# Hybrid decoder layer on one core: the transposes of the last attention gate placed inside the first output unit, seven-product pairs at places 3 to 13

## The chip, the core and the metric

The kernel runs on one core of a Trainium2 chip. TensorE (PE) multiplies matrices, VectorE (DVE) and ScalarE (ACT) work elementwise, GpSimd (POOL) and SyncE (SP) here only issue DMAs. The metric is the device time of one execution in microseconds, lower is better. Before the change it is 1550.36 us, the median of 3 runs (1549.83 to 1550.70).

## What is computed

One decoder layer on 256 tokens of width 4096, in float32: an RMS norm, one input projection to eight parts, three mixers (pooling, stick-breaking attention, a state space), each normalised and gated, and one output projection with the residual, then a last RMS norm.

```python
def hybrid_layer(x, ...):
    h = rmsnorm(x, ln_g)
    p_x, p_gate, q, k, v, a_gate, s_u, s_gate = jnp.split(h @ w_in, ...)
    y_pool = pool_mixer(p_x, ...)
    y_attn = stick_breaking_attention(q, k, v)
    y_ssm = s5_mixer(s_u, ...)
    y_pool = rmsnorm(y_pool, g_pool) * jax.nn.silu(p_gate)
    y_attn = rmsnorm(y_attn, g_attn) * jax.nn.silu(a_gate)
    y_ssm = rmsnorm(y_ssm, g_ssm) * jax.nn.silu(s_gate)
    y = jnp.concatenate([y_pool, y_attn, y_ssm], axis=-1)
    return x + y @ w_out
```

## The kernel before

The weights are cut into pieces of 128 x 2 x 512 numbers (512 KB). A list `subs` holds all 528 pieces in the order of use, and one loop walks through it. In each step the loop issues the loads that come due (on SP's queue, four pieces ahead, six in the output part), splits the piece after next into a high and a low part, and issues the step's matmuls. The split is `hi_lo`: ACT makes `hi` as a rounded copy, the DVE makes `lo` as the difference. A product in float32 is three matmuls (hi x hi, lo x hi, hi x lo), so a plain piece takes 12 matmuls: two rows of the piece, two token halves, three products. The split parts lie in a ring of 4 buffers, 6 in the output part.

The pieces form units. 24 input units and 4 GLU units come first, the last of them the four units `ag` of the attention gate. Then come four output units `out`, each 16 places `s` with two pieces (`h` = 0, 1) and 1024 columns of the result. In an output unit some places, listed in `SEVEN`, multiply their two pieces as a 2 x 2 block with seven products instead of eight: 21 matmuls instead of 24, for which `split_seven` makes four sums of weight halves (the tile named `t`, in a loop of its own on the DVE), and `row_sums` makes three sums of the token side (`ts`, then the split `y`). `row_difference` overwrites a half of the place's rows with a difference, so such a place can no longer be multiplied plainly. The products `p7` (four halves of PSUM banks, printed as `p`) gather over all such places of a unit, and `join_seven` adds them up (the tile `e`) after the last one, then into `o`; at the end of the unit `finish` adds the accumulator `pm` to `o`.

The stationary side of the output units is `xhl`, 32 slots of 128 channels, split. The gated branches `y` are transposed on TensorE (`transposed`, 8 transposes in two halves `h`) into a PSUM tile `ps_t`. The first seven groups of four slots go to DRAM (`kept`) and come back in the last `ag` unit (`take_back`, tile `yk`, at every second step of it). The last attention gate (`ag` unit 3) has no time for that: `direct` writes slots 28 to 31 from `ps_t` straight into `xhl`. They are read by the places 14 and 15.

That gate is a generator, `att_gate`, with four steps: load `ya` and form the sigmoid `sgm` on ACT and DVE; multiply into `ya`; first half of the transposes; second half. Generators stand in `side_q`; `pump` runs steps of the first one, `drain` runs all to their end. Before the change, `drain(side_q)` stands directly behind the last `ag` unit's matmuls. Engines other than SP take their instructions in the order that a scheduler gives at build time; SP takes them as written. Within an engine the order is kept at run time, so an instruction that waits holds up all behind it.

PSUM has 8 banks. In the output part four tiles `b0` to `b3` of two banks each divide them: unit `n` gathers in two of them (`pm`) and puts its seven products (`p7`) in the other two, and the next unit swaps the pairs. The first output unit takes `b0`, `b1` for `pm`, over the banks of the `ag` units' accumulators.

The buffers tagged `k4` (six) are shared by `agz`, `ya`, `sgm`, `yk`, the sums `t7`, `fg` and `e7`.

At the very end, the last `HELD` = 4 pieces are multiplied for the first token half only, and for the second half after that, so that the first half's result is normalised and stored while TensorE still works.

Of the kernel before, what the change touches and what calls it, by code (L numbers as in the profile page):

```python
# [12 lines left out]
F32 = mybir.dt.float32  # L13
# [7 lines left out]
P = 128  # L21
L = 256
D = 4096
KT = D // P
NU = 512
# [9 lines left out]
RING_OUT = 6  # L35
K4 = 6
LATE_AT = 15
SEVEN = (2, 4, 6, 8, 10, 12)
WIDE = 2 * NU
WARM = 8  # L40
SQUARE_AT = (0, 1, 3, 4, 6, 7, 9, 10)
# [17 lines left out]
OUT_FROM = 24 * 16 + 4 * 4  # L59
# [3 lines left out]
def body(tc, a, out, ctx):  # L63
    nc = tc.nc
# [18 lines left out]
    bp = pool("base")  # L83
# [74 lines left out]
    def hi_lo(dst_hi, dst_lo, src):  # L158
        made = act(dst_hi, src, AF.Copy)
        tt(dst_lo, src, dst_hi.bitcast(F32), ALU.subtract)  # L160
        return made
# [10 lines left out]

    def seven(i):
        ui, s, h = subs[i]
        return units[ui][0] == "out" and s in SEVEN

    def flat(w):
        return w.rearrange("p k n -> p (k n)")
# [61 lines left out]
    def row_sums(where, kept_in, s, xa, xb):  # L240
        t = where.tile([P, 3, P], F32, tag="t", bufs=1, name="ts")
        tt(t[:, 0, :], xa[:, P:L], xb[:, P:L], ALU.add)
        tt(t[:, 1, :], t[:, 0, :], xa[:, 0:P], ALU.subtract)
        tt(t[:, 2, :], xb[:, 0:P], t[:, 1, :], ALU.subtract)
        y = where.tile([P, 3, 2, P], F32R, name="y7_%d" % s)
        hi_lo(y[:, :, 0, :], y[:, :, 1, :], t)
        kept_in[s] = y

    def row_difference(xa):
        tt(xa[:, P:L], xa[:, 0:P], xa[:, P:L], ALU.subtract)  # L250
# [13 lines left out]
    state = {"s7_out": {}, "out": False}  # L264
# [33 lines left out]

    def transposed(y, emit):
        for h in range(2):  # L300
            ps = pk.tile([P, 512], F32, tag="ps", bufs=2, name="ps_t")
            for c in range(2):
                for t in range(2):
                    T.transpose(ps[:, (c * 2 + t) * P:(c * 2 + t + 1) * P], y[:, t, (h * 2 + c) * P:(h * 2 + c + 1) * P], ident)  # L304
            for c in range(2):
                emit(h * 2 + c, ps[:, c * L:c * L + L])
            yield
# [19 lines left out]
    def take_back(g):  # L327
        t = bp.tile([P, 4, L], F32, tag="k4", bufs=K4, name="yk")
        nc.sync.dma_start(t, kept[g])
        for h in range(2):  # L330
            s = 2 * g + h
            if s in SEVEN:
                row_sums(state["out_rows"], state["s7_out"], s, t[:, 2 * h, :], t[:, 2 * h + 1, :])
                row_difference(t[:, 2 * h, :])
        hi_lo(xhl[:, 4 * g:4 * g + 4, 0, :], xhl[:, 4 * g:4 * g + 4, 1, :], t)

    def square_sums(dst, y, n):
        junk = mp.tile([P, 512], BF16, tag="junk", bufs=1, name="junk")
# [366 lines left out]
    def pump(q, n):  # L705
        while q and n > 0:
            try:
                if next(q[0], "end") == "end":
                    q.popleft()
                    continue  # L710
            except StopIteration:
                q.popleft()
                continue
            n -= 1

    def drain(q):
        pump(q, 1 << 30)
# [47 lines left out]

    def start_end():
        nonlocal ep
        drain(side_q)
        late_ctx.close()
        psum_ctx.close()  # L770
        ep = end_ctx.enter_context(tc.tile_pool(name="end", bufs=1, side="right", reuse_waits="tile"))
        state["o"] = ep.tile([P, 2, D], F32, name="o")
        state["po"] = end_ctx.enter_context(tc.tile_pool(name="pout", bufs=1, space=PSUM, reuse_waits="tile"))
        state["out"] = True

    def start_out(n):
        if n == 0:
            start_end()
        four = [state["po"].tile([P, 2, NU], F32, tag="b%d" % j, bufs=1, name="pm" if j // 2 == n % 2 else "p7") for j in range(4)]
        c, p = four[n % 2 * 2:n % 2 * 2 + 2], four[2 - n % 2 * 2:4 - n % 2 * 2]  # L780
        o = state["o"][:, :, n * WIDE:n * WIDE + WIDE]
        for h in range(2):
            nc.sync.dma_start(o[:, :, h * NU:h * NU + NU], a["xr"][2 * n + h])
        return c, p, o

    def load_fg(n):
        fg = bp.tile([P, WIDE], F32, tag="k4", bufs=K4, name="fg")
# [91 lines left out]
    for i, (ui, s, h) in enumerate(subs):  # L879
        kind, c, nk = units[ui]  # L880
        if ui == 1 and s == 0:
            constants()
        if ui == 1 and s in SQUARE_AT:
            square_x(SQUARE_AT.index(s))
        if ui == 1 and s == 12:
            with tc.high_priority():
                norm_x()
                take_u(scaled(state.pop("ps0"), "suz"), 0)
        if s == 0 and h == 0:
            if ui == LATE_AT:  # L890
                start_late()
            if kind == "out":
                ps, pp, state["o_n"] = start_out(c)
                pp = [pp[j // 2][:, j % 2, :] for j in range(4)]
            else:
                ps = [pm.tile([P, NU], F32, tag="c%d" % t, bufs=2, name="pm") for t in range(2)]
            if kind == "glu" and hhl is None:
                hhl = split_glu()
        while loaded < min(len(subs), i + 1 + LOAD_AHEAD + (2 if state["out"] else 0)):
            if loaded == 0:  # L900
                load_first()
            else:
                if loaded < KT // 2:
                    load_x(loaded)
                load(loaded)
            loaded += 1
        while split_to < min(len(subs), i + 1 + SPLIT_AHEAD):
            split(split_to)
            split_to += 1
        if kind == "ag" and c == A_G + 1536 and s >= 2 and s % 2 == 0:  # L910
            take_back(s // 2 - 1)
        rows = hhl if kind == "glu" else xhl
        if seven(i):
            if h == 0:
                mm_seven(i, s, ps, pp, s == SEVEN[0], s == SEVEN[-1])
                if s == SEVEN[-1]:
                    state["fg"] = load_fg(c)
                    state["joined"] = join_seven(pp, state["o_n"])
        else:
            pair = htiles.pop(i)  # L920
            late = i >= N_SUB - HELD
            into = [ps[t][:, h, :] for t in range(2)] if kind == "out" else ps
            mm_tok(into, rows, (2 * s, 2 * s + 1), pair, s == 0, s == nk // 2 - 1, (0,) if late else (0, 1))
            if late:
                delayed.append((s, h, pair))
        if s == nk // 2 - 1 and h == (1 if kind == "out" else 0):
            n = nth.get(kind, 0)
            nth[kind] = n + 1
            if (kind, n) != ("out", 3):
                finish(kind, c, n, ps)  # L930
            if kind == "ag" and n == 3:
                drain(side_q)
        pump(side_q, 3)
        if i >= SSM_FROM:
            want = (i - SSM_FROM) * SSM_RATE
            while ssm_steps[0] < want and ssm_q:
                pump(ssm_q, 1)
                ssm_steps[0] += 1
# [121 lines left out]
```

## Time and profile before

| | |
|---|---|
| median of 3 runs | 1550.36 us |
| the profiled execution | 1550.4 us |
| its span in the trace | 1548.6 us |
| mean granted clock of TensorE | 0.992 |
| last matmul of the last `ag` unit starts | 1180.80 us |
| first matmul of the first output unit starts | 1198.66 us |
| end of the output units' matmuls | 1537.2 us |

The span is what the trace covers; the 1.8 us between it and the time lie around it. Busy times of engines run side by side. A row of the timeline has start, duration, engine, line, operation, written tile <- read tiles, shapes, a count, and in brackets the idle time before it with what ended it. Durations overlap a little: the next instruction of an engine starts before the former one's end, so the cost of a row is the distance between starts. A row of the stretches (windows) has the stretch, its length, the busy times of the engines with counts, the granted clock, the DMA share and GB/s.

### The profile page before, as it was taken

How to read it: one execution, taken by the hardware profiler on the slowest of the kernel's cores; microseconds unless marked ns; L12 is line 12 of the kernel's file. 1: busy time of each engine (PE TensorE's matmuls, PEld its weight loads, DVE VectorE, ACT ScalarE, POOL GpSimd, SP SyncE). 2: the span in 40 equal slices, each digit the busy share in tenths (PEclk: the TensorE clock that was granted, in tenths of full speed). 3: DMA queues.
4: the chain of work that ended last, by engine and by line, in shares of the span. 5: the costliest groups of instructions: out<-in, count | busy, mean ns of one | idle time of the engine just before them, and what ended most of it. 6: DMA issues, size and time to landing. Idle time of an engine off the chain costs nothing.

```text
span 1548.6 us, 19301 instructions
## 1 busy us (share of the span) xinstructions
PE 1517.0 (98%) x6896; PEld 1243.1 (80%) x6896; DVE 1148.9 (74%) x1729; ACT 854.0 (55%) x1118; POOL 10.5 (1%) x23
## 2 busy tenths in 40 slices
PE   9999999999999999999999999999995999999996
PEld 7888888888787888888888888888884888888885
DVE  7579878898988978897544444655558789898977
ACT  7654546665554655565545444745556555655554
POOL 0000000000000000000000000000000000000000
PEclk9999999999999999999999999999998999999998
DMA  9866656566666556655555655676667575666655
GB/s 356 308 214 207 193 176 212 187 218 206 213 201 191 187 169 208 194 170 177 185 190 164 201 187 180 198 243 217 217 218 274 172 240 198 222 219 216 204 185 190
DMA packets 98528, 321.70 MB, mean 208 GB/s; under 512 B 12160, under 2 KB 18048, under 8 KB 98432
## 3 DMA queue, kind: packets, MB, share of 16 engines
q1 hardware_dynamic: 85552, 299.59, 58.4%
q10 hardware_dynamic: 10144, 10.92, 2.4%
q0 software_dynamic: 2736, 9.96, 1.7%
q8 instruction: 54, 0.88, 0.2%
q14 instruction: 42, 0.34, 0.1%
HBM read 306.27 MB, written 11.01 MB: 205 GB/s over the span
## 4 chain that ended last, share of the span: by engine, by line
PE 97%; DVE 1%; ACT 1%; DMA 0%; issue 0%; SPq 0%; DVEq 0%
PE pm L259 28%; PE pm L260 28%; PE pm L261 28%; PE p L227 4%; PE pm L227 3%; PE ps_y L599 1%; PE ps_c L693 1%; PE ps_t L304 1%; PE ps_bu L572 0%; PE ps_p L381 0%; PE ps_z L624 0%; DMA w<-in_ws 0%; PE ps_z L642 0%; PE ps_p L373 0%; PE ps_av L654 0%
## 5 line engine op out<-in xcount | busy, mean ns | idle before, releaser
L92 DVE TENSOR_TENSOR lo<-w,hi 128x1024 fp32r<-128x1024 f32 (+1 forms) x499 | 595.2, 1197 | 315.3 <-ACT hi L104 313.2
L104 ACT ACTIVATE hi<-w 128x1024 fp32r<-128x1024 f32 (+1 forms) x499 | 515.9, 1038 | 489.7 <-PE pm L261 452.0
L260 PE MATMUL pm<-lo,xhl 128*128 128x512 f32 x1856 | 725.7, 391 | 0.0
L261 PE MATMUL pm<-hi,xhl 128*128 128x512 f32 x1856 | 725.2, 391 | 0.0
L259 PE MATMUL pm<-hi,xhl 128*128 128x512 f32 x1856 | 719.7, 391 | 2.4 <-ACT hi L104 0.9
L259 PEld LDWEIGHTS pm<-hi,xhl 128*128 128x128 f32 x1856 | 348.8, 188 | 78.3 <-issue 2.9
L260 PEld LDWEIGHTS pm<-lo,xhl 128*128 128x128 f32 x1856 | 348.9, 188 | 74.0 <-issue 2.5
L261 PEld LDWEIGHTS pm<-hi,xhl 128*128 128x128 f32 x1856 | 348.9, 188 | 73.7 <-issue 2.1
L104 ACT ACTIVATE hi<-t 128x1024 fp32r<-128x1024 f32 x48 | 50.9, 1061 | 25.4 <-ACT hi L104 7.5
L92 DVE TENSOR_TENSOR lo<-t,hi 128x1024 fp32r<-128x1024 f32 x48 | 58.3, 1221 | 4.9 <-ACT hi L104 4.7
L101 DVE SCALAR_TENSOR_TENSOR et<-et,pw,tr 128x16 f32<-128x16 f32 (+3 forms) x256 | 55.5, 275 | 2.0 <-ACT tr L104 1.8
L104 ACT ACTIVATE tr<-et,pw 128x32 f32<-128x32 f32 (+3 forms) x128 | 44.1, 382 | 11.1 <-DVE et L101 6.8
L104 ACT ACTIVATE hi<-o 128x1024 fp32r<-128x1024 f32 (+1 forms) x32 | 30.7, 978 | 32.5 <-PE pm L261 30.6
L92 DVE TENSOR_TENSOR lo<-o,hi 128x1024 fp32r<-128x1024 f32 (+1 forms) x32 | 35.4, 1122 | 12.0 <-ACT hi L104 11.7
L587 DVE TENSOR_TENSOR_SCAN tb<-rho,ta 128x256 f32<-128x256 f32 x64 | 40.6, 676 | 0.3
L227 PE MATMUL p<-hi,y 128*128 128x512 f32 x96 | 37.6, 391 | 0.0
L227 PE MATMUL pm<-hi,xhl 128*128 128x512 f32 x96 | 37.6, 391 | 0.0
L227 PE MATMUL p<-hi,xhl 128*128 128x512 f32 x96 | 37.6, 391 | 0.0
L92 DVE TENSOR_TENSOR t<-w 128x512 f32<-128x512 f32 x36 | 23.4, 688 | 15.1 <-DMA w<-in_ws 14.6
L104 ACT ACTIVATE sgm<-sgm 128x1024 f32<-128x1024 f32 x24 | 25.3, 1053 | 4.0 <-DVE sgm L101 3.8
L259 PE MATMUL pm<-hi,hhl 128*128 128x512 f32 x64 | 25.1, 398 | 0.7 <-DVE gl L92 0.7
L261 PE MATMUL pm<-hi,hhl 128*128 128x512 f32 x64 | 25.2, 394 | 0.0
(244 smaller groups left out, 1082.4 us busy)
## 6 DMA issues: line engine op xcount, KB each, us to landing
w<-in_ws SPq DMA_DIRECT2D x495, 512.0 KB, 3.7
o<-in_ws SPq DMA_DIRECT2D x32, 512.0 KB, 4.5
xsq<-in_xr SPq DMA_DIRECT2D x8, 512.0 KB, 6.6
o<-in_xr SPq DMA_DIRECT2D x8, 512.0 KB, 6.8
xt<-in_xT SPq DMA_DIRECT2D x15, 256.0 KB, 6.2
kept<-yT POOLq DMA_DIRECT2D x7, 512.0 KB, 4.7
yk<-kept SPq DMA_DIRECT2D x7, 512.0 KB, 6.0
b<-in_bst ACTq DMA_DIRECT2D x16, 192.0 KB, 4.8
```

What stands on the lines that cost most here:

```text
L92: V.tensor_tensor(o, x, y, op)
L101: V.scalar_tensor_tensor(o, x, s, y, op0, op1)
L104: return S.activation(o, x, f, **kw)
L227: T.matmul(o, stat[:, p, :], pair[q][:, n], start=start and k == 0, stop=stop and k == 2, skip_group_check=True)
L259: T.matmul(ps[t], stat[:, slot, 0, sl], hi[:, n], start=begin, stop=False, skip_group_check=True)
L260: T.matmul(ps[t], stat[:, slot, 0, sl], lo[:, n], start=False, stop=False, skip_group_check=True)
L261: T.matmul(ps[t], stat[:, slot, 1, sl], hi[:, n], start=False, stop=end, skip_group_check=True)
L304: T.transpose(ps[:, (c * 2 + t) * P:(c * 2 + t + 1) * P], y[:, t, (h * 2 + c) * P:(h * 2 + c + 1) * P], ident)
L587: V.tensor_tensor_scan(tb[:, c, :], rho[:, pr:pr + 1].broadcast_to([P, L]), ta[:, c, :], 0.0, ALU.mult, ALU.add)
L599: T.matmul(ps[32 * j:32 * j + 32, 0:L], cf[:, j, c, :], ss[j][:, c, :], start=c == 0, stop=c == 1, skip_group_check=True)
L693: T.transpose(ps[:, (c * 2 + t) * P:(c * 2 + t + 1) * P], z[:, t, (h * 2 + c) * P:(h * 2 + c + 1) * P], ident)
```

## The change

`SEVEN` moves from the places 2, 4, ... 12 to 3, 5, ... 13. The first output unit leaves out the first of them and has five (`sevens_of`). The generator of the last gate is no longer run to its end behind the `ag` unit; the loop runs one step of it at the steps listed in `GATE_AT`, counted from the first step of the output part: the sigmoid at -1, the multiplication at 0, the halves of the transposes at 6 and 7 (place 3). As the old side PSUM pool is closed by then, the halves use the tiles `b2` and `b3`, which the unit's seven products take over at its first seven-product place; what is left in `side_q` is drained there. The rows of place 3 must be plain for the first unit and differences for the later ones: `rows_again` reads half a group back from `kept` after the unit's place 5 and makes sums and difference then.

```diff
-SEVEN = (2, 4, 6, 8, 10, 12)
+SEVEN = (3, 5, 7, 9, 11, 13)
+GATE_AT = (-1, 0, 6, 7)
...
-        return units[ui][0] == "out" and s in SEVEN
+        return units[ui][0] == "out" and s in sevens_of(units[ui][1])
+
+    def sevens_of(n):
+        return SEVEN if n else SEVEN[1:]
...
     def transposed(y, emit):
         for h in range(2):
-            ps = pk.tile([P, 512], F32, tag="ps", bufs=2, name="ps_t")
+            if state["out"]:
+                ps = state["po"].tile([P, 2, NU], F32, tag="b%d" % (2 + h), bufs=1, name="ps_t")[:, 0, :]
+            else:
+                ps = pk.tile([P, 512], F32, tag="ps", bufs=2, name="ps_t")
...
-            if s in SEVEN:
+            if s in SEVEN[1:]:
                 row_sums(state["out_rows"], state["s7_out"], s, t[:, 2 * h, :], t[:, 2 * h + 1, :])
                 row_difference(t[:, 2 * h, :])
...
+    def rows_again(s):
+        t = bp.tile([P, 2, L], F32, tag="k4", bufs=K4, name="yk")
+        nc.sync.dma_start(t, kept[s // 2][:, s % 2 * 2:s % 2 * 2 + 2, :])
+        row_sums(state["out_rows"], state["s7_out"], s, t[:, 0, :], t[:, 1, :])
+        row_difference(t[:, 0, :])
+        hi_lo(xhl[:, 2 * s, 0, P:L], xhl[:, 2 * s, 1, P:L], t[:, 0, P:L])
...
     def start_end():
         nonlocal ep
-        drain(side_q)
...
-        four = [state["po"].tile([P, 2, NU], F32, tag="b%d" % j, bufs=1, name="pm" if j // 2 == n % 2 else "p7") for j in range(4)]
-        c, p = four[n % 2 * 2:n % 2 * 2 + 2], four[2 - n % 2 * 2:4 - n % 2 * 2]
+        c = [state["po"].tile([P, 2, NU], F32, tag="b%d" % (n % 2 * 2 + t), bufs=1, name="pm") for t in range(2)]
...
+    def products(n):
+        p = [state["po"].tile([P, 2, NU], F32, tag="b%d" % (2 - n % 2 * 2 + t), bufs=1, name="p7") for t in range(2)]
+        return [p[j // 2][:, j % 2, :] for j in range(4)]
...
-                mm_seven(i, s, ps, pp, s == SEVEN[0], s == SEVEN[-1])
+                if s == sevens_of(c)[0]:
+                    drain(side_q)
+                    pp = products(c)
+                mm_seven(i, s, ps, pp, s == sevens_of(c)[0], s == SEVEN[-1])
...
-            if kind == "ag" and n == 3:
-                drain(side_q)
-        pump(side_q, 3)
+        if kind == "out" and c == 0 and (s, h) == (SEVEN[0] + 2, 1):
+            rows_again(SEVEN[0])
+        if i < OUT_FROM - 1:
+            pump(side_q, 3)
+        elif i - OUT_FROM in GATE_AT:
+            pump(side_q, 1)
```

The order of instructions that the scheduler makes of it changes at these places. First TensorE, where the last `ag` unit ends and the first output unit begins, before the change (`pm_9715` is an accumulator of the `ag` unit, `pm_10130` one of the output unit):

```order
L259 MATMUL pm_9715<-hi_10024,xhl_102 128x512
L260 MATMUL pm_9715<-lo_10025,xhl_102 128x512
L261 MATMUL pm_9715<-hi_10024,xhl_102 128x512
L304 MATMUL ps_t_10102<-ident_80,ya_10091 128x128 x4
L304 MATMUL ps_t_10111<-ident_80,ya_10091 128x128 x4
L259 MATMUL pm_10130<-hi_10042,xhl_102 128x512
L260 MATMUL pm_10130<-lo_10043,xhl_102 128x512
L261 MATMUL pm_10130<-hi_10042,xhl_102 128x512
```

TensorE in the changed kernel, at the same place and, further on, at the ends of the output unit's pieces 6 and 7, counted from 0 (`pm_10101` and `pm_10102` belong to the output unit):

```order
L263 MATMUL pm_9715<-hi_10016,xhl_102 128x512
L264 MATMUL pm_9715<-lo_10017,xhl_102 128x512
L265 MATMUL pm_9715<-hi_10016,xhl_102 128x512
L263 MATMUL pm_10101<-hi_10034,xhl_102 128x512
L264 MATMUL pm_10101<-lo_10035,xhl_102 128x512
...
L264 MATMUL pm_10102<-lo_10184,xhl_102 128x512
L265 MATMUL pm_10102<-hi_10183,xhl_102 128x512
L311 MATMUL ps_t_10234<-ident_80,ya_10083 128x128 x4
L263 MATMUL pm_10101<-hi_10200,xhl_102 128x512
...
L265 MATMUL pm_10102<-hi_10200,xhl_102 128x512
L311 MATMUL ps_t_10261<-ident_80,ya_10083 128x128 x4
```

The transposes have left the seam between the units: the first four now stand behind piece 6, the other four behind piece 7. Next the DVE over the same stretch, before the change (`sgm` is the sigmoid, `ya` the gated rows, `t` the weight sums of the first seven-product place):

```order
L101 SCALAR_TENSOR_TENSOR sgm<-agz,sgm 128x1024
L92 TENSOR_TENSOR ts<-ts,yk 128x128
L92 TENSOR_TENSOR yk<-yk 128x128
L92 TENSOR_TENSOR t_10176<-o 128x512 x2
L92 TENSOR_TENSOR ts<-yk,ts 128x128
L92 TENSOR_TENSOR t_10177<-o,t_10176 128x512
L92 TENSOR_TENSOR xhl<-yk,xhl 128x4x256
L101 SCALAR_TENSOR_TENSOR ya<-ya,r_b_9047,agz 128x512 x2
L92 TENSOR_TENSOR t_10177<-o,t_10177 128x512
L92 TENSOR_TENSOR lo<-t_10176,hi 128x1024
L92 TENSOR_TENSOR y_12_10052<-ts,y_12_10052 128x3x128
L92 TENSOR_TENSOR ya<-ya,sgm 128x1024
```

and in the changed kernel (the `lo` are those of the pieces 4, 5 and 6, then 7 to 9):

```order
L102 SCALAR_TENSOR_TENSOR sgm<-agz,sgm 128x1024
L93 TENSOR_TENSOR ts<-ts,yk 128x128
L93 TENSOR_TENSOR yk<-yk 128x128
L93 TENSOR_TENSOR lo<-o,hi 128x1024
L93 TENSOR_TENSOR ts<-yk,ts 128x128
L93 TENSOR_TENSOR xhl<-yk,xhl 128x4x256
L102 SCALAR_TENSOR_TENSOR ya<-ya,r_b_9047,agz 128x512 x2
L93 TENSOR_TENSOR lo<-o,hi 128x1024
L93 TENSOR_TENSOR lo<-w,hi 128x1024
L93 TENSOR_TENSOR y_13_10044<-ts,y_13_10044 128x3x128
L93 TENSOR_TENSOR ya<-ya,sgm 128x1024
L93 TENSOR_TENSOR lo<-w,hi 128x1024 x3
```

The weight sums of the first seven-product place have gone to a later point, and splits of plain pieces stand in their place, around the rows of the gate. Last the DVE at the end of the kernel, before the change (`e` is the join of the seven products, `o<-pm` the first result of the final addition):

```order
L92 TENSOR_TENSOR lo<-w,hi 128x1024 x4
L92 TENSOR_TENSOR e_12634<-e_12633,p_12098 128x512
L92 TENSOR_TENSOR lo<-w,hi 128x1024
L92 TENSOR_TENSOR e_12633<-e_12634,p_12097 128x512
L92 TENSOR_TENSOR lo<-w,hi 128x1024
L92 TENSOR_TENSOR e_12634<-e_12634,p_12098 128x512
L92 TENSOR_TENSOR o<-o,e_12633 128x1024
L92 TENSOR_TENSOR e_12634<-e_12634,p_12097 128x512
L92 TENSOR_TENSOR o<-o,e_12634 128x1024
L92 TENSOR_TENSOR o<-pm,o 128x512 x2
```

and in the changed kernel:

```order
L93 TENSOR_TENSOR lo<-w,hi 128x1024 x4
L93 TENSOR_TENSOR e_12661<-e_12660,p_12223 128x512
L93 TENSOR_TENSOR e_12660<-e_12661,p_12222 128x512
L93 TENSOR_TENSOR e_12661<-e_12661,p_12223 128x512
L93 TENSOR_TENSOR o<-o,e_12660 128x1024
L93 TENSOR_TENSOR e_12661<-e_12661,p_12222 128x512
L93 TENSOR_TENSOR o<-o,e_12661 128x1024
L93 TENSOR_TENSOR o<-pm,o 128x512 x2
```

The join now stands behind the last split, with no split between its rows, since only two places follow the last seven-product place.

More of the change, by code (lines that the diff above doesn't have):

```diff
@@ L783, in start_out @@
             nc.sync.dma_start(o[:, :, h * NU:h * NU + NU], a["xr"][2 * n + h])
-        return c, p, o
+        return c, o
+    def products(n):
+        p = [state["po"].tile([P, 2, NU], F32, tag="b%d" % (2 - n % 2 * 2 + t), bufs=1, name="p7") for t in range(2)]
+        return [p[j // 2][:, j % 2, :] for j in range(4)]
     def load_fg(n):
@@ L892, in body @@
             if kind == "out":
-                ps, pp, state["o_n"] = start_out(c)
-                pp = [pp[j // 2][:, j % 2, :] for j in range(4)]
+                ps, state["o_n"] = start_out(c)
             else:
```

## The prediction

> **What bounds the kernel now.** I read the page's head and slices first, then the waits of TensorE, then the stretches around the one dip.
>
> ```profile
> span 1548.6 us, 19301 instructions
> PE 1517.0 (98%) x6896; PEld 1243.1 (80%) x6896; DVE 1148.9 (74%) x1729; ACT 854.0 (55%) x1118; POOL 10.5 (1%) x23
> ...
> PE   9999999999999999999999999999995999999996
> ...
> PEclk9999999999999999999999999999998999999998
> ...
> PE 97%; DVE 1%; ACT 1%; DMA 0%; issue 0%; SPq 0%; DVEq 0%
> ```
>
> TensorE is busy in 98% of the span and the chain that ended last is TensorE for 97%. So matmul time is the time, and anything else counts only where TensorE stands still. There is one such place before the end: slice 31, where the busy digit falls to 5 and the clock digit to 8.
>
> ```profile
> PE ps_t L304 <- DVE ya L92: 15.9, 1, 15.9
> ```
>
> That is the first row of TensorE's waits: one wait of 15.9 us, of the transposes of `ya` for the DVE that makes `ya`. The next one in that answer is 1.2 us. The stretches show what the other engines did meanwhile:
>
> ```profile
> 1100.00:1181.03 81.03, 81.03 (x367) 67.09 (x365) 49.91 (x59) 45.46 (x54) 2.14 (x4) 1.00 0.76 261
> 1181.03:1202.53 21.50, 5.63 (x18) 4.70 (x18) 19.89 (x32) 12.64 (x17) 0.00 (x0) 0.60 0.38 150
> ...
> 1300.00:1500.00 200.00, 200.00 (x873) 163.46 (x872) 169.08 (x183) 109.46 (x116) 0.00 (x0) 1.00 0.63 209
> ```
>
> Columns: the stretch and its length, then busy time of PE, PEld, DVE, ACT, POOL, the granted clock, DMA share and GB/s. In the middle stretch TensorE works 5.63 of 21.50 us at a granted clock of 0.60 while the DVE works 19.89 of it. In the output units (last row) TensorE never stops, and the DVE is at 169.08/200 = 85%: it is the engine that could become the bound next.
>
> **What goes: the wait and the slow clock behind it.**
>
> ```profile
> 1150.90 1.03 PE L304 MATMUL ps_t<-ident,ya 128*128 128x128 f32 x8
> ...
> 1151.69 0.48 PE L259 MATMUL pm<-hi,xhl 128*128 128x512 f32 x1
> ...
> 1152.01 0.40 PE L260 MATMUL pm<-lo,xhl 128*128 128x512 f32 x1
> ...
> 1180.80 0.39 PE L261 MATMUL pm<-hi,xhl 128*128 128x512 f32 x1
> 1197.06 1.94 PE L304 MATMUL ps_t<-ident,ya 128*128 128x128 f32 x8 [15.87 <-DVE ya L92]
> 1198.66 0.78 PE L259 MATMUL pm<-hi,xhl 128*128 128x512 f32 x1
> ...
> 1202.53 0.39 PE L259 MATMUL pm<-hi,xhl 128*128 128x512 f32 x1
> ```
>
> Matmuls start every 0.227 us at full clock: the stretch from piece to piece below gives 5.46 us for 24. The last one of the gate unit starts at 1180.80, so the next could start at 1181.03; the transposes start at 1197.06: **16.03 us**. The eight transposes then take 1198.66 - 1197.06 = 1.60 us, where the same eight in the gate before, at full clock, took 1151.69 - 1150.90 = 0.79: **0.81 us**. The nine matmuls from 1198.66 to 1202.53 take 3.87 us instead of 9 x 0.227 = 2.04: **1.83 us**. With the wait gone, TensorE never idles, so the clock has no reason to fall: it was 1.00 over the whole stretch before. Together 18.67 us.
>
> [...]
>
> **Can TensorE really run on at 1181.03?** Five things must be ready. I count the pieces (one load of 128x1024 weights) of the first output unit from 0, twelve matmuls = 2.72 us each, so piece n is due at 1181.03 + 2.72 n.
>
> ```profile
> 1180.10 0.69 ACT L104 ACTIVATE agz<-pm,rtok 128x512 f32<-128x512 f32 x1 [1.27 <-PE pm L261]
> ...
> 1181.63 0.68 ACT L104 ACTIVATE agz<-pm,rtok 128x512 f32<-128x512 f32 x1
> ...
> 1189.70 1.04 ACT L104 ACTIVATE xhl<-yk 128x1024 fp32r<-128x1024 f32 x1
> ...
> 1183.63 1.22 DVE L92 TENSOR_TENSOR lo<-w,hi 128x1024 fp32r<-128x1024 f32 x1
> ...
> 1187.48 1.22 DVE L101 SCALAR_TENSOR_TENSOR sgm<-agz,sgm 128x1024 f32<-128x1024 f32 x1
> ...
> 1188.82 0.28 DVE L92 TENSOR_TENSOR yk<-yk 128x128 f32<-128x128 f32 x1
> 1189.02 1.29 DVE L92 TENSOR_TENSOR t<-o 128x512 f32<-128x512 f32 x2
> ...
> 1192.17 1.41 DVE L101 SCALAR_TENSOR_TENSOR ya<-ya,r_b,agz 128x512 f32<-128x512 f32 x2
> ...
> 1195.70 1.22 DVE L92 TENSOR_TENSOR ya<-ya,sgm 128x1024 f32<-128x1024 f32 x1
> 1196.83 1.29 DVE L92 TENSOR_TENSOR t<-w 128x512 f32<-128x512 f32 x2
> ```
>
> 1) The PSUM of the unit, freed by the two `agz`: the first half at 1180.79, before it is due; the second at 1182.31, due after six matmuls at 1182.39. Nothing, at most 0.1 us. 2) Splits of pieces 0 to 3: they stand before this point in both orders and were done by 1185 (the row at 1183.63 is the last), due 1189.2 at the latest. 3) Piece 4 and 5: up to 1189.02 the DVE's order is the same in kind; there it now takes the `lo` of piece 4 (1.13 us from its start to that of the next row, as 1195.70 to 1196.83) instead of `t`: ready 1190.2, due 1191.9. Then `ts` 0.2, `xhl` from 1190.8 (it waits for ACT's row at 1189.70 to end), two `ya` 1.3, and `lo` of piece 5 from 1193.2: ready 1194.5, due, with the second matmul of the piece, 1194.9. This is the **tightest place, 0.3 us**. 4) `lo` of piece 6 (1195.6, due 1197.4), `y` 0.5, then the product `ya` (1.14): ready 1197.2. The transposes now stand behind piece 6, at 1200.1: 2.9 us in hand. 5) `lo` of 7, 8, 9 by 1200.5 (piece 7 due 1200.5, and its lo first, at 1198.3), then the first seven-product pair (pieces 10, 11), due at 1181.03 + 27.2 + 0.9 = 1209.1. In front of its parts stand five `t` and `lo` rows and three of the four `xhl<-ps_t`; its raw `lo` comes at 1202.9, `low` at 1205.2, `high` at 1209.4, due 1212.5. The last `xhl<-ps_t` ends at 1209.9; the bank that it frees is due 1212. So the DVE is busy without a break from 1181.8 to 1209.9, but TensorE should not stand. I count **0 us**, bounds 0 (all hidden) and 4 us (an estimate: 0.15 us of extra hand-off on each of some 25 rows of the DVE, all of it ending on TensorE).
>
> The split transposes break the row of matmuls once more: behind the eight, the matmul at 1151.69 was followed by one at 1152.01, after 0.32 instead of 0.227 us, so **+0.1 us**.
>
> **What comes: one pair fewer in seven products.**
>
> ```profile
> 1211.40 0.39 PE L227 MATMUL p<-hi,xhl 128*128 128x512 f32 x1
> ...
> 1216.24 0.39 PE L259 MATMUL pm<-hi,xhl 128*128 128x512 f32 x1
> ...
> 1221.70 0.39 PE L227 MATMUL p<-hi,xhl 128*128 128x512 f32 x1
> ```
>
> A seven-product pair takes 1216.24 - 1211.40 = 4.84 us (21 matmuls), a plain one 5.46 us (24). The first unit has five places instead of six: **+0.62 us**. The DVE has less to do there, so its 85% does not rise.
>
> **What is read back.** Row sums of pair 3 are made after its plain use, from a second read of `kept`. Six small DVE rows and two of ACT; all but the split of 128x128 (one row on each, about 0.28 us) replace those of pair 2. The DMA stands on SP behind the loads of pieces 16 and 17, which wait until the DVE has left pieces 10 and 11 (1206.3): issue about 1207.
>
> ```profile
> DMA to landing us min/median/max: 5.4/6.0/7.8
> ```
>
> That row is of the seven earlier read-backs, of twice the size. With 6.0 it lands at 1213.0; the DVE comes to it at 1212.1 and waits 0.9 us. Behind it on the DVE stands `lo` of piece 13, then ready at 1214.4 and due 1216.7; even 7.8 us (ready 1216.2) stays hidden. The built program lists no wait at this DMA, so the loads behind it on SP are not held. **0 us**; without that cover, one us for each us of landing beyond 8.2.
>
> **The ends of the units come one pair later.** The join now has two plain pairs, 10.9 us, before the next unit writes the same banks, not three.
>
> ```profile
> 1267.83 0.68 DVE L92 TENSOR_TENSOR e<-e,p 128x512 f32<-128x512 f32 x1
> ...
> 1274.16 0.68 DVE L92 TENSOR_TENSOR e<-e,p 128x512 f32<-128x512 f32 x1
> ```
>
> The pair ended about 1267.7 (five periods of 4.84 + 5.46 after 1216.24); the fourth `e`, the last to read the first bank, ended at 1274.84, 7.1 us later, in nearly the order that the DVE has now. Hidden, 3.8 us in hand. At the last unit nothing follows but the end:
>
> ```profile
> 1519.50 0.39 PE L259 MATMUL pm<-hi,xhl 128*128 128x512 f32 x1
> ...
> 1524.96 0.39 PE L259 MATMUL pm<-hi,xhl 128*128 128x512 f32 x1
> ...
> 1518.89 2.48 DVE L92 TENSOR_TENSOR lo<-w,hi 128x1024 fp32r<-128x1024 f32 x2 [0.59 <-ACT hi L104]
> ...
> 1526.17 0.68 DVE L92 TENSOR_TENSOR e<-e,p 128x512 f32<-128x512 f32 x1
> ...
> 1528.62 1.23 DVE L92 TENSOR_TENSOR o<-o,e 128x1024 f32<-128x1024 f32 x1
> 1530.67 1.29 DVE L92 TENSOR_TENSOR o<-pm,o 128x512 f32<-128x512 f32 x2 [0.83 <-PE pm L261]
> ...
> 1534.20 0.50 PE L259 MATMUL pm<-hi,xhl 128*128 128x512 f32 x1 [0.78 <-DVE o L92]
> ...
> 1537.30 0.69 DVE L92 TENSOR_TENSOR o<-pm,o 128x512 f32<-128x512 f32 x1 [0.31 <-PE pm L261]
> ```
>
> The seven-product pair ended at 1519.50, and the last four pieces began a whole pair later, at 1524.96; `o<-pm` came 5.71 us after that. Now the four pieces begin at once. Their last `lo` ends, as that of the two rows at 1518.89 did, 1.8 us after the pair; then two `e` (1.25) and the rest of the join, which took from 1526.17 to the end of the row at 1528.62, 1529.85: 3.68 us: `o<-pm` starts 6.7 us after the pair, 1.0 us later than before. The DVE works on without a gap to the last `o<-pm`, so the end moves by about **+1.0 us** (from 0, if the join finds gaps, to 1.5).
>
> **The sum.** The profiled execution took 1550.4 us (span 1548.6 and 1.8 around it), 0.04 above the median 1550.36, so no correction. 1550.4 - 18.67 + 0.1 + 0.62 + 1.0 = **1533.5 us**, 1.1% less.
>
> **Rivals.** *The DVE becomes the bound in the first output unit.* For it: 28 us without a break and 0.3 us in hand at piece 5. Against: the later places have 2 us and more. It gives 1 to 4 us of waits, and half clock on top only where one wait is long: 1535.5 to 1538. *The read-back comes late and the DVE stands before it, with the splits behind.* Doubled to 12 us it costs 3.8: 1537.3. *This goes on to the other side*: SP's loads share the queues, and if the read-back took 8.2 + 16.9 = 25 us, the DVE's wait would eat the whole gain, and beyond that the kernel is slower, say 1555 at 30 us plus the clock's fall. Against: the maximum of seven is 7.8 us, DMA share 0.6. *The transposes wait in their new place*: the product `ya` would have to be 2.9 us late before it costs, 19.8 us before it loses. That the change does not do what it says is excluded: in the order the first output matmul follows the last gate matmul.
>
> **Chances.** Forecast (1531.5 to 1535.5) 0.66; DVE bound 0.17; read-back or transposes late, still faster 0.10; within 0.2% (3.1 us, about what a measurement of this kernel can tell) 0.03; slower 0.03; below 1531.5 0.01. The range 1531.5 to 1539 takes in the DVE's bound and part of the late read-back. Faster 0.94.
>
> **What would show it.** The 15.9 us wait is gone from TensorE's waits and slice 31 reads 9 with clock 9; the transposes come in two groups of four near 1200.1 and 1203.3, without a wait; the first `p` at 1209; the last `o<-pm` 17 us earlier than 1537.30. Wrong if TensorE's waits list a new row over 1 us: `pm<-lo` on the DVE at piece 5 (first rival), or a DVE wait on DMA for `yk` followed by one of TensorE (second).

## The result, and the profile after

The changed kernel takes **1534.22 us** (median of four runs, 1533.5 to 1534.45) against 1550.37 (four runs, 1549.83 to 1550.7): a ratio of **0.9895**, 95% interval 0.9878 to 0.9913. The forecast was 1533.5 us within 1531.5 to 1539.0. The profiled execution of the changed kernel took 1534.27 us, with a span of 1532.5.

The head, two of the slices and the chain's first line, from the page of the changed kernel. Its lines are numbered up to 14 higher than before: the three plain matmuls of a piece are L263 to L265, those of a seven-product pair L231, the transposes L311.

```profile
span 1532.5 us, 19305 instructions
...
PE 1517.0 (99%) x6899; PEld 1243.5 (81%) x6899; DVE 1143.9 (75%) x1724; ACT 851.0 (56%) x1117; POOL 10.5 (1%) x23
...
PE   9999999999999999999999999999999999999996
...
PEclk9999999999999999999999999999999999999998
...
PE 98%; DVE 1%; ACT 0%; DMA 0%; issue 0%; DVEq 0%; ACTq 0%
```

The matmuls take as long as before (1517.0 us busy); the span around them has shrunk by 16.1. The dip in slice 31 is gone from both rows. TensorE's waits in the changed kernel, the longest first (engine, tile, line, what it waited for, then us in total, times, longest):

```profile
PE ps_i L122 <- DVE zeros L119: 1.2, 1, 1.2
PE pm L263 <- DVE ss_out L975: 0.8, 1, 0.8
PE pm L263 <- DVE gl L93: 0.7, 1, 0.7
PE pm L263 <- ACT xhl L105: 0.6, 1, 0.6
```

The row of 15.9 us has no successor: each of these four has its like in the kernel before, within 0.1 us, and the second stands at the very end. TensorE's timeline of the changed kernel around the seam (start, duration, instruction):

```profile
1181.75 0.39 PE L265 MATMUL pm<-hi,xhl 128*128 128x512 f32 x1
1181.98 0.40 PE L263 MATMUL pm<-hi,xhl 128*128 128x512 f32 x1
...
1183.35 0.45 PE L263 MATMUL pm<-hi,xhl 128*128 128x512 f32 x1
1183.64 0.39 PE L264 MATMUL pm<-lo,xhl 128*128 128x512 f32 x1
...
1201.22 0.60 PE L311 MATMUL ps_t<-ident,ya 128*128 128x128 f32 x4
...
1204.46 0.60 PE L311 MATMUL ps_t<-ident,ya 128*128 128x128 f32 x4
...
1210.39 0.39 PE L231 MATMUL p<-hi,xhl 128*128 128x512 f32 x1
```

The last matmul of the gate (1181.75) and the first of the output unit (1181.98) are one step apart. The seventh, which needs the second half of the PSUM, loses 0.06 us (0.29 to the next where a step is 0.23). The transposes stand in two groups without a wait, and the row of the stretch says the same in one line (length, then busy time of PE, PEld, DVE, ACT, POOL, the granted clock, DMA share, GB/s):

```profile
1181.05:1203.00 21.95, 21.95 (x99) 17.93 (x98) 19.57 (x27) 17.16 (x21) 0.00 (x0) 1.00 0.69 244
```

TensorE is busy for all of the 21.95 us, at a granted clock of 1.00 where it was 0.60. The DVE works 19.57 us there, where it was 19.89 us in the stretch of the kernel before; that work is now done beside the matmuls.

**A measure that is finer than the median.** TensorE's work ahead of the seam is the same in every kernel here, yet the first `agz` of the last gate began anywhere from 1179.15 to 1181.05 us (the last section traces it for two executions of one kernel). So I compare from the first `agz` to the last `o<-pm`, and quote both ends where it matters: before, 1180.10 to 1537.30, 357.20 us; after, 1181.05 to 1521.22, 340.17 us. The change is **-17.03 us**; the forecast's terms sum to -16.95. From the last `o<-pm` to the end of the span both kernels take 11.3 us.

### The profile page after: what moved, and what is told of

It is laid out like the page before. It is cut to its first block, busy times and chain, and to the rows that moved or that the text cites. A ratio compares the mean times of both kernels' runs of the same rounds, so it can differ in the third digit from the quotient of the medians.

```text
span 1532.5 us, 19305 instructions
## 1 busy us (share of the span) xinstructions
PE 1517.0 (99%) x6899; PEld 1243.5 (81%) x6899; DVE 1143.9 (75%) x1724; ACT 851.0 (56%) x1117; POOL 10.5 (1%) x23
## 4 chain that ended last, share of the span: by engine, by line
PE 98%; DVE 1%; ACT 0%; DMA 0%; issue 0%; DVEq 0%; ACTq 0%
PE pm L263 29%; PE pm L264 29%; PE pm L265 29%; PE p L231 4%; PE pm L231 3%; PE ps_y L613 1%; PE ps_c L707 1%; PE ps_bu L586 1%; PE ps_t L311 0%; PE ps_p L395 0%; PE ps_z L638 0%; PE ps_z L656 0%; DMA prm<-in_prm 0%; PE ps_p L387 0%; PE ps_av L669 0%; PE ps_av L668 0%
## 5 line engine op out<-in xcount | busy, mean ns | idle before, releaser
L265 PE MATMUL pm<-hi,xhl 128*128 128x512 f32 x1864 | 727.9, 391 | 0.0
L263 PE MATMUL pm<-hi,xhl 128*128 128x512 f32 x1864 | 722.6, 392 | 1.4 <-DVE ss_out L975 0.8
L263 PEld LDWEIGHTS pm<-hi,xhl 128*128 128x128 f32 x1864 | 350.5, 188 | 77.5 <-issue 2.9
L265 PEld LDWEIGHTS pm<-hi,xhl 128*128 128x128 f32 x1864 | 350.5, 188 | 74.3 <-issue 2.1
L231 PE MATMUL p<-hi,y 128*128 128x512 f32 x92 | 36.0, 391 | 0.0
L231 PE MATMUL pm<-hi,xhl 128*128 128x512 f32 x92 | 36.0, 391 | 0.0
L231 PE MATMUL p<-hi,xhl 128*128 128x512 f32 x92 | 36.0, 391 | 0.0
L263 PE MATMUL pm<-hi,hhl 128*128 128x512 f32 x64 | 25.1, 398 | 0.7 <-DVE gl L93 0.7
L265 PE MATMUL pm<-hi,hhl 128*128 128x512 f32 x64 | 25.2, 394 | 0.0
```

Source lines behind the costliest of these rows:

```text
L231: T.matmul(o, stat[:, p, :], pair[q][:, n], start=start and k == 0, stop=stop and k == 2, skip_group_check=True)
L263: T.matmul(ps[t], stat[:, slot, 0, sl], hi[:, n], start=begin, stop=False, skip_group_check=True)
L265: T.matmul(ps[t], stat[:, slot, 1, sl], hi[:, n], start=False, stop=end, skip_group_check=True)
```

## Experiments

### 1. The transposes moved, the pairs left where they were

```diff
-SEVEN = (3, 5, 7, 9, 11, 13)
+SEVEN = (2, 4, 6, 8, 10, 12)
```

> The changed kernel with the places 2, 4, ... 12 (4, ... 12 in the first output unit): the gate is inside the unit, the places are not shifted. My theory: the seam is gone as in the changed kernel, but the first seven-product pair is due 5.4 us earlier, before the DVE has its sums, splits and the reads of the transposes done, so TensorE waits there for the DVE, about 4 us for the first bank and 2 us for the second; the late shift at the end of the kernel (0.7 us) is not paid. Expected 1538 to 1541 us with two new waits of the products on the DVE. Rival (the shift of the places is not needed, only its price at the end is paid): 1532.5 to 1533.8 us and no wait over 1 us.

Measured: 1533.49 us, ratio 0.9889 (0.9874 to 0.9903), span 1531.6; first `agz` to last `o<-pm` 340.54 us (1179.86 to 1520.40). **My expectation missed**: I had looked for a wait of several microseconds where the first pair needs the transposed rows. TensorE's timeline of this kernel in the first output unit:

```profile
1206.70 0.40 PE L263 MATMUL pm<-hi,xhl 128*128 128x512 f32 x1
1207.42 0.50 PE L231 MATMUL pm<-lo,xhl 128*128 128x512 f32 x1 [0.33 <-DVE lo L93]
...
1209.61 0.40 PE L231 MATMUL p<-hi,xhl 128*128 128x512 f32 x1
```

The order is not the one in which the code is written. Where the products into `p` would have stood, TensorE runs the `pm` products of the pair and the plain products of the next pieces, and the first `p` comes at 1209.61, 29.75 us behind the first `agz`, about where the changed kernel has it (1210.39, 29.34 behind). All that is left as a wait is one step of 0.72 us instead of 0.23. The rival had it right: 1532.5 to 1533.8 us and no wait over 1 us. So the gain comes without the later places of the pairs; these are worth 0.4 us net (340.54 against 340.17). Gross it is some 1.1: this kernel's end is that of the kernel before (from the matmul behind the last pair to the last `o<-pm` 17.82 us, 1502.58 to 1520.40, where before it was 17.80), so it is spared the 0.69 us that the change costs at the end, and loses it and 0.4 more elsewhere. Nearly all of that is in the first output unit: from its first matmul to that of the next unit it takes 86.37 us (1180.80 to 1267.17), in the changed kernel 85.35 (1181.98 to 1267.33), 1.02 less. The step of 0.72 shows 0.49 of it; the rest is spread over slightly longer steps of many matmuls, and their cause stays open.

### 2. The pairs moved, the transposes left where they were

The kernel before with the tuple of places changed, and nothing else:

```diff
-SEVEN = (2, 4, 6, 8, 10, 12)
+SEVEN = (3, 5, 7, 9, 11, 13)
```

> The kernel before with the places 3, 5, ... 13 in all four units, the transposes still at the seam. My theory: the whole gain is the seam, so the wait of the transposes for the DVE stays at 15 to 17 us with the half clock behind it, and the end costs some 0.7 us: 1550 to 1552.5 us. Rival (the shift itself relieves the DVE at the seam, and part of the gain is that): the wait falls to 12 us or less and the time to 1546.5 us or less.

Measured: 1551.94 us, ratio 1.0012 (1.0003 to 1.0021). TensorE's timeline of this kernel still has the wait at the seam:

```profile
1197.10 1.94 PE L304 MATMUL ps_t<-ident,ya 128*128 128x128 f32 x8 [16.82 <-DVE ya L92]
```

By the finer measure it loses 1.81 us (1179.18 to 1538.19, 359.01): 0.95 at this wait, 16.82 for 15.87, and most of the rest at the end: from the first matmul behind the last pair to the last `o<-pm` it takes 13.15 us (1525.04 to 1538.19). In the kernel before, the last four pieces began at 1524.96 and the last `o<-pm` came 12.34 us later: 0.81 more. The pairs' new places cost something at the end, and gain nothing alone.

### 3. The wait kept, the clock kept up through it

The kernel before, with 64 matmuls between the last gate matmul and the transposes whose results nothing reads:

```diff
+        fill = pk.tile([P, 512], F32, tag="ps", bufs=2, name="ps_f")
+        for _ in range(FILL):
+            T.matmul(fill, htiles[i + 1][0][:, 0:P], htiles[i + 1][0][:, 0:NU], start=True, stop=True)
         drain(side_q)
```

> The kernel before, with 64 additional matmuls (128x512, on a split piece that is ready, into a spare PSUM tile that nothing reads) in TensorE's order between the last gate matmul and the transposes: they fill about 14.5 of the 16 us, so TensorE still waits for the same rows but does not fall idle. My theory: the transposes start where they did (about 16 us after the last gate matmul), and they and the nine matmuls behind them run at full clock: 2.6 us less than before, 1547.4 to 1548.2 us. [...] If the slow start were not the clock but cold operands: no change, 1550.4 us.

Measured: 1548.13 us, ratio 0.9985 (0.9976 to 0.9995); by the finer measure 354.69 us (1179.50 to 1534.19), **2.51 us less** than before. TensorE's timeline of this kernel at the seam:

```profile
1180.43 14.67 PE L935 MATMUL ps_f<-hi 128*128 128x512 f32 x64
...
1196.48 1.06 PE L305 MATMUL ps_t<-ident,ya 128*128 128x128 f32 x8 [1.38 <-DVE ya L93]
1197.30 0.47 PE L260 MATMUL pm<-hi,xhl 128*128 128x512 f32 x1
```

The transposes come as late as before, but eight of them now take 0.82 us (1196.48 to 1197.30) instead of 1.60, and the matmuls behind them keep their step. The two terms for the slow clock were 0.81 + 1.83 = 2.64 us, and the run gives 2.51 of it. The granted clock says the same. In the kernel before it is 0.50 from 1185.34 to 1202.40 us; the last 5.34 us of that, from the start of the transposes, are a loss of 2.67 us at half rate. In this run it is 1.00 from 1180 to 1203 us. So the slow start was the clock and not cold operands.

Half clock lasts 17.06 us in the kernel before: 11.72 of the wait and 5.34 of the work behind it. By the steps of the matmuls, the last slow one (0.43 us) ends 5.16 us behind the start of the transposes there (1197.06 to 1202.22), and 5.58 us behind it in the kernel of experiment 2 (1197.10 to 1202.68). What sets these lengths no run here shows.

### 4. One seven-product pair fewer in the second unit too

```diff
-        return SEVEN if n else SEVEN[1:]
+        return SEVEN if n > 1 else SEVEN[1:]
...
-        if kind == "out" and c == 0 and (s, h) == (SEVEN[0] + 2, 1):
+        if kind == "out" and c == 1 and (s, h) == (SEVEN[0] + 2, 1):
```

> The changed kernel with five instead of six seven-product places in the second output unit too (place 3 is plain there, and its read-back comes in that unit). My theory: one more plain pair costs TensorE 5.46 - 4.84 = 0.62 us and nothing else: 1534.6 to 1535.1 us, span 0.4 to 0.9 us longer than that of the changed kernel. Rival (the DVE is near its limit, and the relief of 4 us of its work per pair gives the 0.6 us back): 1534.2 us or less.

Measured: 1534.10 us, ratio 0.9893 (0.9878 to 0.9908). The median missed the expected 1534.6 to 1535.1 and lies where the rival had it, but a median of four runs cannot tell so little: the first `agz` of this execution came 0.51 us earlier than the changed kernel's. By the finer measure it takes 340.93 us (1180.54 to 1521.47), **0.76 more** than the changed kernel. The term in the forecast was 5.46 - 4.84 = 0.62. With the read-back now in the second unit, TensorE's waits of that kernel get no new row either.

### 5. The end: who is late at the last sum

The forecast put +1.0 us at the end down to the join. The trace after (below, in the section on the forecast) pointed at two other things: ACT squares half of the second block of rows ahead of the first block's norm, and the DVE scales the first block ahead of the last sum. The first run puts the square behind the norm's last activation; the second also puts the last sum ahead of the scaling and its store.

```diff
-        act(dst, t, AF.Exp, scale=-0.5)
+        state["exp"] = act(dst, t, AF.Exp, scale=-0.5).ins.name
...
+            if (t, h) == (1, 0):
+                tc.add_manual_dep(sq.ins, state["exp"], ...)
```

> The changed kernel with one order on ACT at the very end: the square of the second token half's first columns stands behind the two small activations of the first half's norm, as it stood before the change, instead of ahead of them. My theory: of the 0.69 us that the end is later (13.03 us from the end of the last seven-product pair to the last o<-pm, 12.34 before), most is the small norm chain waiting for ACT (0.87 us of idle DVE ahead of rs_t), not the join of the products: from that pair to the last o<-pm 12.4 to 12.7 us, 0.35 to 0.6 us less in the stretch from the last gate matmul to the end. Rival (the join behind the last split is what delays the end, as the prediction had it): no change, 13.0 us.

Measured: 1532.68 us, ratio 0.9887 (0.9870 to 0.9903). From the matmul behind the last pair to the last `o<-pm`, 12.68 us (1506.91 to 1519.59) instead of 13.03. ACT's timeline of that kernel:

```profile
1516.27 0.20 ACT L105 ACTIVATE rs_t<-rs_m 128x1 f32<-128x1 f32 x1 [1.12 <-DVE rs_m L99]
1516.51 0.20 ACT L105 ACTIVATE r_out<-rs_t 128x1 f32<-128x1 f32 x1
1516.61 0.61 ACT L105 ACTIVATE e<-o 128x512 f32<-128x512 f32 x1
```

The square, in the last row, now follows the two small activations of the norm. For the second run the added lines are:

```diff
+            added = V.tensor_tensor(last[:, t, cols], ps[t][:, h, :], last[:, t, cols], ALU.add)
+            if (t, h) == (1, 1):
+                made = V.scalar_tensor_tensor(o[:, 0, held[1]], o[:, 0, held[1]], held[2], fg, ALU.mult, ALU.mult)
+                tc.add_manual_dep(made.ins, added.ins.name, ...)
+                nc.sync.dma_start(out[held[0], held[1]], o[:, 0, held[1]])
...
+                if t == 0:
+                    held = (rows, cs, r)
+                    continue
```

> As the run before, and in addition the DVE does the last sum o<-pm before the last scaling of the first token half (1.2 us), which then follows it, with its store. My theory: the last sum then waits for TensorE alone and starts 0.2 us after its last matmul ends, 12.2 us after the last seven-product pair: 0.8 us less than the changed kernel in the stretch from the last gate matmul to the last sum, and as much at the end if the stores (the last of them is another one) don't give it back. Rival (the end is set by the stores of the first half, which now come later): the last sum moves, the end does not.

Measured: 1532.46 us, ratio 0.9887 (0.9872 to 0.9902). The DVE's timeline of that kernel:

```profile
1519.06 0.69 DVE L970 TENSOR_TENSOR o<-pm,o 128x512 f32<-128x512 f32 x1 [0.66 <-PE pm L265]
1519.67 1.28 DVE L972 SCALAR_TENSOR_TENSOR o<-o,r_out,fg 128x1024 f32<-128x1024 f32 x1
```

The last sum now waits for TensorE (0.66 us), 12.22 us behind the pair's end (1506.84 to 1519.06). The end is back at TensorE, where it was before the change (12.34). But the delayed scaling now stands ahead of the second block's norm: from the last `o<-pm` to the end of the span it takes 11.64 us instead of 11.3, so of the 0.81 us gained at the sum 0.35 is given back. From the first `agz` to the end of the span (the end less the first `agz`), the changed kernel takes 351.45 us, the first of these runs 351.13 and the second 351.00.

### 6. The gate's steps placed earlier

```diff
-GATE_AT = (-1, 0, 6, 7)
+GATE_AT = (-1, 0, 2, 3)
```

> The changed kernel with the halves of the transposes called at the steps 2 and 3 of the output part instead of 6 and 7. In the order of the built program all eight transposes still stand behind piece 6, since the scheduler knows that ya is not there earlier. My theory: no difference beyond 0.2 us in the stretch from the last gate matmul to the last o<-pm (170 to 171 us shorter or longer by no more than that), because no wait arises. Rival (the place in the code sets the place on TensorE): the transposes wait for the DVE behind piece 2 for some 8 us with the clock falling, 1542 us or more.

Measured: 1533.11 us (two runs), ratio 0.9889 (0.9869 to 0.9909); first `agz` to last `o<-pm` 340.12 us (1179.32 to 1519.44), the changed kernel's time to 0.05. TensorE's timeline of that kernel:

```profile
1198.54 1.03 PE L311 MATMUL ps_t<-ident,ya 128*128 128x128 f32 x8
1199.33 0.48 PE L265 MATMUL pm<-hi,xhl 128*128 128x512 f32 x1
```

There is still no wait, though the eight now stand as one group and 0.95 us earlier in the unit (19.22 us behind the first `agz`, where the first group of the changed kernel stands 20.17 behind it). So the place has slack, and splitting the transposes into two groups costs no more than 0.05 us.

### 7. Both once more, side by side

The medians of the kernels with a new order at the end lay 1.5 to 1.8 us below the changed kernel's, four times as much as their ends showed. So the changed kernel and the second order of the end ran again, side by side on one chip.

> The changed kernel once more, on the same chip as the next one, to tell a difference of about half a microsecond at the end from the one microsecond by which the unchanged stretch ahead of the seam moves from build to build and run to run. If that stretch moves by run, 1533 to 1534.5 us here, and the first agz to the last o<-pm takes 340.1 to 340.3 us again. If it was a property of one build, the first agz starts at 1181.0 again.

> The order with the square behind the norm and the last sum ahead of the scaling, once more. If its gain is only what the end shows, the span from the first agz to the end is 0.3 to 0.6 us shorter than in the changed kernel of the same call and the median 0.3 to 0.6 us lower. If the earlier distance of 1.8 us between the medians was the order's, 1.5 us lower again.

Measured: 1532.93 us (0.9892, 0.9875 to 0.9908) for the changed kernel, just below the 1533 to 1534.5 expected, and 1533.07 (0.9891, 0.9876 to 0.9906) for the other. The finer measure repeats itself: 340.15 us (1179.15 to 1519.30) and 339.33 (1180.92 to 1520.25), where it was 340.17 and 339.36. The first `agz` does not repeat: 1179.15 where the same kernel had 1181.05, and 1180.92 where the other had 1179.70. So that offset belongs to the execution, not to the build, and the earlier distance of the medians was mostly this. From the first `agz` to the end of the span the new order takes 350.98 us against 351.45: 0.47 less, as at first (0.45). The expected difference of the medians, 0.3 to 0.6 us, did not show (+0.14); a median of four runs cannot tell it.

## Why the forecast held, step by step

**The wait and the slow clock (18.67 us).** Right. Experiment 2 shows that the pairs' new places alone do not remove the wait, experiment 1 that the transposes' new place does so without them, and experiment 3 measures the clock's part as 2.51 us against 2.64. The rows after agree. From the first `agz` to the first output matmul it took 18.56 us (1180.10 to 1198.66) and takes 0.93 (1181.05 to 1181.98): 17.63 less, the 16.03 of the wait and the 1.60 of the slow transposes. These come back inside the unit as two groups of 0.36 and 0.35 us, at 1201.22 and 1204.46, where I had 0.79 for all eight.

**The transposes split in two (+0.1 us), and the way to the first pair.** The first `p` stands 28.41 us behind the first output matmul (1181.98 to 1210.39), where the forecast had 28.1. The split is not the cause: experiment 6 bounds it at 0.05 us. Each group does cost more than its own time, since the matmul behind it takes 0.32 us to the next one, and 0.06 us went at the second half of the PSUM. The remainder lies in the step itself: from 1205.13 to 1207.67, 11 matmuls of the changed kernel take 2.54 us, 0.231 each, where I had reckoned 0.227 throughout. Why it is 0.231 there was not tried, but it is no cost of the change. With the transposes ahead of the unit and the clock kept up (experiment 3), the first output unit takes 83.83 us for 366 matmuls (1197.30 to 1281.13), 0.229 each. The changed kernel's takes 85.35 us for 369 and the transposes; less 0.79 + 0.1 for these it is 0.229 each again.

**One pair fewer in seven products (+0.62 us).** Right: 0.76 when done once more (experiment 4).

**The DVE (0 us, and the tightest place 0.3 us in hand).** Right in the 0 us; there was more in hand. Its timeline in the changed kernel:

```profile
1189.98 1.22 DVE L93 TENSOR_TENSOR lo<-o,hi 128x1024 fp32r<-128x1024 f32 x1
...
1194.20 1.22 DVE L93 TENSOR_TENSOR lo<-o,hi 128x1024 fp32r<-128x1024 f32 x1
...
1196.95 1.22 DVE L93 TENSOR_TENSOR ya<-ya,sgm 128x1024 f32<-128x1024 f32 x1
...
1213.05 0.29 DVE L93 TENSOR_TENSOR ts<-yk 128x128 f32<-128x128 f32 x1
```

The first two rows are the splits of pieces 4 and 5. The forecast had the second start at 1193.2, with the unit starting at 1181.03; the unit here starts at 1181.98, so that start is one of 1194.15, and the row has 1194.20. It ends at 1195.42, and the second matmul of piece 5 is due at 1181.98 + 13.6 + 0.2 = 1195.8. That would leave the foretold 0.3 us. The row had more in hand than that, for TensorE runs a second product with `hi` ahead of the first one with `lo`, which starts at 1196.15, 0.73 us after that end:

```profile
1195.70 0.61 PE L263 MATMUL pm<-hi,xhl 128*128 128x512 f32 x2
1196.15 0.39 PE L264 MATMUL pm<-lo,xhl 128*128 128x512 f32 x1
```

The upper bound of 4 us rested on 0.15 us of hand-off a row, which no row shows; this start came within 0.05 us of where I had it, some fifteen rows into the unit. The product `ya` ends at 1198.17, 3.05 us ahead of the first transposes. The rival in which the DVE becomes the bound of the first unit did show itself, but in experiment 1: 0.33 us of waiting for a `lo`, with the pairs in the old places.

**The read-back (0 us).** Right, and with more room than I gave it. SP's queue and the tile's answer in the changed kernel:

```profile
1208.16 0.42 SPq L346 DMA_DIRECT2D yk<-kept  x1
...
DMA to landing us min/median/max: 4.3/6.1/7.2
```

Issued at 1208.16, it is there when the DVE comes to it: the row `ts<-yk` at 1213.05 has no wait in brackets, where I had one of 0.9 us.

**The end (+1.0 us).** Mis-sized, and by the wrong mechanism: this is the step that failed. I had the last splits end 1.8 us behind the pair and the join start there. The DVE's timeline of the changed kernel:

```profile
1504.69 3.67 DVE L93 TENSOR_TENSOR lo<-w,hi 128x1024 fp32r<-128x1024 f32 x3 [1.49 <-ACT hi L105]
1508.28 2.12 DVE L93 TENSOR_TENSOR e<-e,p 128x512 f32<-128x512 f32 x3
...
1514.30 1.29 DVE L93 TENSOR_TENSOR o<-pm,o 128x512 f32<-128x512 f32 x2 [0.90 <-PE pm L265]
...
1518.37 0.16 DVE L93 TENSOR_TENSOR rs_t<-r_out,rs_m 128x1 f32<-128x1 f32 x1 [0.87 <-ACT r_out L105]
...
1520.02 1.28 DVE L102 SCALAR_TENSOR_TENSOR o<-o,r_out,fg 128x1024 f32<-128x1024 f32 x1
1521.22 0.69 DVE L93 TENSOR_TENSOR o<-pm,o 128x512 f32<-128x512 f32 x1
```

The pair's last matmul is followed by the next at 1508.19, and the join starts at 1508.28: it is not late, and the first `o<-pm` waits for TensorE, not for the join. It comes 6.11 us behind the pair (before: 5.71; forecast: 6.7), for two more matmuls stand ahead of the one that it waits for: that one starts at 1513.87, the 26th of the stretch, where in the kernel before it was the 24th (1530.24). These are most likely two of the second token half; their steps are 2 x 0.227 = 0.45 us. From there to the last `o<-pm` it is 6.92 us where it was 6.63. In the last row there is no wait: TensorE was done (its last matmul starts at 1519.96 and ends at 1520.35), and the DVE came late. It had waited 0.87 us for the norm's activations, since ACT took a square first, and it scaled a block ahead of the sum:

```profile
1517.29 0.63 ACT L105 ACTIVATE e<-o 128x512 f32<-128x512 f32 x1 [0.87 <-DVE o L93]
1517.83 0.19 ACT L105 ACTIVATION_READ_ACCUMULATOR e<-o 128x1 f32 x1
1517.92 0.19 ACT L105 ACTIVATE rs_t<-rs_m 128x1 f32<-128x1 f32 x1
1518.14 0.20 ACT L105 ACTIVATE r_out<-rs_t 128x1 f32<-128x1 f32 x1
```

These are ACT's rows of the changed kernel; experiment 5 turned the order round. The square accounts for 0.35 us and the scaling for 0.46 at the last sum, together more than the +0.69 us that the change cost there (13.03 against 12.34). That 1.0 lay near 0.69 was luck: what it was reckoned from did not happen.

**The sum.** -18.67 + 0.1 + 0.62 + 1.0 was -16.95; measured, -17.03. By stages the change is -17.63 us up to the first output matmul; -0.23 in the first output unit (85.58 to 85.35, where 1.83 of slow clock has gone and 0.79 of transposes has come, so 0.81 is left for the pair and the split, against 0.72 foretold); +0.16 in the second and third unit together (167.86 to 168.02), where I had nothing; and +0.67 from the first matmul of the last unit to the last `o<-pm` (85.20 to 85.87, against 1.0). So part of the close agreement is luck: 0.33 us too much at the end stands against 0.25 too little ahead of it. The four-run median of 1534.22 lies 0.7 above the forecast and the repeated one of 1532.93 0.6 below it; both are within the offset of the start of an execution.

## What to carry to other kernels

Where the engine that bounds a kernel waits for a chain on another engine, put independent matmuls between the last input of that chain and its use, and count both the wait and the slow stretch behind it: here 16.0 and 2.6 us. Read the order from the built program and not from the code before a wait is foretold, since a scheduler may already put other work there, as in experiment 1. For differences below 0.1% measure between two events that enclose the change: that repeated within 0.03 us where the whole executions moved by two.

## What the hardware showed unexpectedly

The same program began its last gate up to 1.9 us earlier or later. The difference is made in the first ten microseconds. TensorE's timeline of the changed kernel in its first profile:

```profile
6.42 1.05 PE L264 MATMUL pm<-lo,xhl 128*128 128x512 f32 x2
...
9.83 0.63 PE L264 MATMUL pm<-lo,xhl 128*128 128x512 f32 x1
10.26 0.52 PE L265 MATMUL pm<-hi,xhl 128*128 128x512 f32 x1
10.62 0.62 PE L263 MATMUL pm<-hi,xhl 128*128 128x512 f32 x2
```

and in its second (experiment 7):

```profile
6.22 0.79 PE L264 MATMUL pm<-lo,xhl 128*128 128x512 f32 x2
6.85 0.63 PE L265 MATMUL pm<-hi,xhl 128*128 128x512 f32 x2
7.32 0.62 PE L263 MATMUL pm<-hi,xhl 128*128 128x512 f32 x2
...
8.70 0.62 PE L263 MATMUL pm<-hi,xhl 128*128 128x512 f32 x2
```

In the first, matmuls start 0.43 us apart up to 10.26 (9.83 to 10.26); in the second they are at 0.23 from 6.85 on (two in 0.47 us). The matmul at 10.62 in the first is the one at 8.70 in the second: 1.92 us, of which 0.20 was there before (6.42 and 6.22), and the first `agz` differs by 1.90. The profile's granted clock reads 1.00 in both stretches, so here the step alone shows the slow matmuls. Why one execution of the kernel has more of them at its start than the other, these two do not show.

The second surprise is the length of the slow stretch after the wait: the clock fell 4.15 us after the last matmul had ended (1181.19 to 1185.34), half clock then lasted 5.34 us into the work, and keeping the array busy through the wait gave 2.51 us back.
